# Pad tiles that move the addresses of matmul operands in a two-layer fp32r backbone

## The chip, the cores and the metric

The kernel runs on one core of a Trainium2 chip. The metric is the device time of one execution in microseconds; less is better. Below, PE is the matrix engine, and PEld is the load of a matmul's stationary operand into it, which the profile lists as an engine of its own. DVE and ACT are the vector and the scalar engine, POOL is GpSimd, and SP is the engine whose queue issues most weight transfers.

## What is computed

Two layers of a post-norm transformer backbone over 256 latent tokens of 2048 channels, with 256 context tokens that only the first layer reads. Layer 0 mixes tokens by neighbourhood attention with 16 heads, layer 1 by a gated MLP with a 128x128 position mix per channel group. A SwiGLU feed-forward block with an inner width of 5632 follows each mixer, and every sub-layer is modulated by shift, scale and gate vectors that are computed from a condition vector. In short:

```python
for i in range(2):
    sh1, sc1, g1, sh2, sc2, g2 = split(silu(c) @ ada_w[i] + ada_b[i], 6)
    a = h * (1 + sc1) + sh1
    y = attention(a, ctx) if i == 0 else gmlp(a)
    h = layer_norm(ALPHA * h + g1 * y)
    m = h * (1 + sc2) + sh2
    gate, up = split(m @ ffn_w_in[i], 2)
    h = layer_norm(ALPHA * h + g2 * ((silu(gate) * up) @ ffn_w_out[i]))
```

All of it is in float32. The kernel keeps that precision by splitting each operand of a large product into two fp32r parts (`hi`, the rounded value, and `lo`, the rest) and adding three products.

## The kernel before

**Products.** `mm3` (lines 88 to 91) issues three matmuls into one PSUM tile: stationary high with moving high (L89), stationary high with moving low (L90), stationary low with moving high (L91). In the blocks after attention the moving operand is 512 columns of a weight tile, and the stationary operand is 128x128 of the activations, split in the same way.

**Pieces.** All weights come through one queue of pieces of 128x1024 floats, in the order in which they are needed. `prefetch` (from line 106) loads a piece by SP's queue into one of four `raw` tiles, and `split_into` (L94 on ACT, L95 on DVE) writes its `hi` and `lo` tiles. There are two sets of these: set A, three pairs in the pool `outer`, and set B, two pairs in the pool `main`, which opens after attention. Pieces go round them by their number modulo 5: three pieces to A, then two to B. At the end of each output projection four half-tiles of a tile called `extra` (`extra_o`, `extra`, `extra_g`) take the place of A and B for the last two of its pieces and for two of the next block's.

**Blocks after attention.** One piece feeds 12 matmuls (two 128-deep slices, two halves of the tokens, three products). In `block_T` (feed-forward input: tiles `pg` and `pu`; gMLP input: `gv` and `gu`) the stationary operand is the modulated activation in `main` (tags `acth`, `actl`; tiles `f0h`, `m1h`, `f1h` and their low parts). In `project_out` (tiles `powo`, `pod`, `pogo`) it is a freshly split 128x256 slice in `outer` (tags `gh`, `gl`). `flip` (L768) transposes the feed-forward's inner activations by four small matmuls at a time. The feed-forward input has 11 blocks of two parts of eight pieces per layer, 176 pieces; the feed-forward output has 88 per layer, the gMLP input 64, and the two mixers' output projections 32 each.

**Fillers.** Between pieces `tick` starts tasks that compute the modulation vectors on DVE from transfers issued by ACT's queue (`ad` at L153, `ag` at L177).

**Addresses.** A pool gives each tag a place that is as large as its largest tile, one after the other in the order of first use, in steps of 32 bytes; pools lie on top of each other as they open. An address here is the byte offset within each partition. In the program of the kernel before:

```
pool   tag or tile             address            modulo 256   modulo 512
outer  xT (extra)              20032              64           64
outer  hi/lo, set A            60992 + n * 4096   64           64
outer  gh, gl                  110144 + n * 1024  64           64
main   h_t (16384 bytes)       118336             64           64
main   ca, cb, st (640 bytes)  134720
main   hi/lo, set B            135360 + n * 4096  192          192
main   acth, actl              155840, 172224     192          192
above  pw: w (extra_o)         192832             64           320
above  ffn: gTb, then sg       192832, 221504     64           320, 320
above  gm: ws, bs              192832, 201024     64           320
above  gm: vv (extra_g)        201088             128          384
```

The slices that a matmul of the blocks after attention reads start at whole multiples of 512 bytes within their tile, so the tile's remainder is the operand's. During attention the weights come from A alone, and the stationary or moving activations lie at 64 modulo 256 too. `ident`, the other operand of the transposes, is at 17408 (0 modulo 256).

Of the kernel before, what the change touches and what calls it, by code (L numbers as in the profile page):

```python
# [12 lines left out]
F32 = mybir.dt.float32  # L13
# [7 lines left out]
P = 128  # L21
# [31 lines left out]
def hybrid_kernel(ctx: ExitStack, tc: tile.TileContext, i, out):  # L53
# [34 lines left out]
    def mm3(ps, sh, sl, mh, ml, first, last, keep=lambda ins: ins):  # L88
        keep(T.matmul(ps, sh, mh, start=first, stop=False))  # L89
        keep(T.matmul(ps, sh, ml, start=False, stop=False))  # L90
        keep(T.matmul(ps, sl, mh, start=False, stop=last))  # L91
# [36 lines left out]
    def piece():  # L128
        prefetch(1)
        got = ready.pop(0)  # L130
        prefetch(pos["bufs"] - 1)
        return got

    def take(k):
        prefetch(k)
        got = ready[:k]
        del ready[:k]
        return got
# [41 lines left out]
    def act_split(src, name, at=None):  # L180
        if at is not None:
            split_into(at[0], at[1], src)
            return at
        gh = outer.tile([P, NT], F32R, tag="gh", name=f"gh{name}", bufs=4)
        gl = outer.tile([P, NT], F32R, tag="gl", name=f"gl{name}", bufs=4)
        split_into(gh, gl, src)
        return gh, gl
# [29 lines left out]
    def tick(n=1.0):  # L217
        fetch_ahead()
        if side:
            side.pop(0)()  # L220
            n *= BUSY
        state["credit"] += n * state["rate"] if tasks else 0.0
        while tasks and state["credit"] >= tasks[0][1]:
            state["credit"] -= tasks[0][1]
            pop_task()
        if not tasks:
            state["credit"] = 0.0

    def need(*keys):
        while any(t[0] in keys for t in tasks):  # L230
            pop_task()
# [46 lines left out]
    with tc.tile_pool(name="attnX", bufs=1) as px, ExitStack() as late:  # L278
# [148 lines left out]
        def acc_tile(name):  # L427
            return mp.tile([P, 512], F32, tag="acc", name=name, bufs=4)

        def s_tile(name):  # L430
            return mp.tile([P, 512], F32, tag="s", name=name, bufs=2)
# [120 lines left out]
    main = ctx.enter_context(tc.tile_pool(name="main", bufs=1))  # L552
    pos["wide"] = main
    pos["bufs"] = 5
    h_t = main.tile([P, 2, D], F32, tag="h", name="h_t")
    nc.sync.dma_start(h_t, i["x_tok"])

    def act_tiles(name):
# [5 lines left out]
    def stats_tile(name):  # L564
        return main.tile([P, 2, NB, 6], F32, tag="st", name=f"st{name}", bufs=2)

    def residual(ps, b, nb, g, st, name):
        sl = slice(nb * 512, (nb + 1) * 512)
        tmp = main.tile([P, 512], F32, tag="tmp", name=f"y{name}{b}{nb}", bufs=2)
        V.tensor_tensor(tmp, ps, g[:, sl], ALU.mult)  # L570
        V.scalar_tensor_tensor(h_t[:, b, sl], h_t[:, b, sl], ALPHA, tmp, ALU.mult, ALU.add)
        V.bn_stats(st[:, b, nb, :], h_t[:, b, sl])
# [12 lines left out]
    def preload_sqrt(st):  # L585
        S.activation(warm, st[:, 0, 0, 0:1], AF.Sqrt)
# [75 lines left out]
    def project_out(kts, src, key, name, finish, extra, last=False):  # L662
        st = stats_tile(name)
        hold = LAST if last else HOLD
        for nh in range(2):
            if nh == 0:
                ps = [[acc_tile(f"po{name}{nh}{n}{b}") for b in range(2)] for n in range(2)]
            else:
                ps = [[s_tile(f"po{name}{nh}0{b}") for b in range(2)]]
                ps.append([acc_tile(f"po{name}{nh}1{b}") for b in range(2)])  # L670

            def products(kt, x, w, n, b):
                c, tb = slice(n * 512, (n + 1) * 512), slice(b * P, (b + 1) * P)
                mm3(ps[n][b], x[0][:, tb], x[1][:, tb], w[0][:, c], w[1][:, c], kt == 0, kt == kts - 1)

            def fetch(kt, n):
                xs = []
                for k in range(n):
                    at = None
                    if k >= START:  # L680
                        if k % 2 == 0:
                            e = outer.tile([P, 4, NT], F32R, tag="ada", name=f"e{name}{k}", bufs=ADA)
                        at = e[:, 2 * (k % 2), :], e[:, 2 * (k % 2) + 1, :]
                    xs.append(act_split(src(kt + k), f"{name}{nh}_{kt + k}", at))
                return xs, take(n)

            k0 = 0
            if nh == 1:
                xs, ws = fetch(0, START)
                for n in range(2):  # L690
                    for j in range(START):
                        for b in range(2):
                            products(j, xs[j], ws[j], n, b)
                preload_sqrt(st)
                k0 = START
            k1 = kts - hold if nh == 1 else kts
            for kt in range(k0, k1):
                if nh == 1 and kt == max(k1 - 9, k0):
                    pos["extra"] = extra()
                w = piece() if nh == 0 or kt < k1 - START else take(1)[0]  # L700
                x = act_split(src(kt), f"{name}{nh}_{kt}")
                for n in range(2):
                    for b in range(2):
                        products(kt, x, w, n, b)
                if nh == 0 or kt < k1 - QUIET:
                    tick()
            if nh == 0:
                need(key)
                g = gate[key]
                for n in range(2):  # L710
                    for b in range(2):
                        residual(ps[n][b], b, n, g, st, name)
            else:
                xs, ws = fetch(k1, hold)
                for b in range(2):
                    for n in range(2):
                        for j in range(hold):
                            products(k1 + j, xs[j], ws[j], n, b)
                        with tc.high_priority(AHEAD):
                            residual(ps[n][b], b, 2 + n, g, st, name)  # L720
                    if not last:
                        with tc.high_priority(AHEAD):
                            finish(b, st)
                if last:
                    for b in range(2):
                        finish(b, st)
# [25 lines left out]
    def ffn(layer, m, key, name, finish, free, last=False):  # L752
# [41 lines left out]
    m = Modulated(0, 0, SH2, SC2, "f0")  # L794
    free = ExitStack()
    pw = free.enter_context(tc.tile_pool(name="pw", bufs=1))
    project_out(
        KT, lambda k: oT[:, k, :], (0, G1), "wo", m.first,
        lambda: pw.tile([P, 4, 1024], F32R, tag="w", name="extra_o"),
# [21 lines left out]
    pg = free.enter_context(tc.tile_pool(name="gm", bufs=1))  # L821
    ws = pg.tile([P, NH, P], F32, tag="ws", name="ws")
    nc.sync.dma_start(ws, i["w_s"])
    bs = pg.tile([P, NH], F32, tag="bs", name="bs")
    nc.sync.dma_start(bs, i["b_s"])
    vv = pg.tile([P, 2, D], F32, tag="vv", name="vv")
    st = stats_tile("v")
    for nb in range(NB):
# [173 lines left out]
```

## Time and profile before

| What | Value |
|---|---|
| time, median of 3 runs | 2493.1 us (2491.81 to 2497.22) |
| the profiled execution's own time | 2484.16 us |
| its span, first to last instruction | 2482.4 us |
| PE busy | 2409.0 us, 97% |
| PEld busy | 1976.3 us, 80% |
| DVE, ACT busy | 1754.9 us (71%), 1118.9 us (45%) |
| mean granted clock of PE | 0.992 |

Busy time of PE is no measure of its pace: matmuls are pipelined, so each one's recorded duration (about 0.39 us for 512 columns) overlaps the next one's. The pace is read from the distance between starts. The 2484.16 us stand 1.8 us above the span, and 0.36% under the median of the runs.

### The profile page before, as it was taken

Reading aid. Unit: us, or ns where it says so; the run is one execution under the profiler, and the core shown is the slowest. Engines: PE = TensorE matmul, PEld = TensorE weight load, DVE = VectorE, ACT = ScalarE, POOL = GpSimd, SP = SyncE. Lnnn points to the kernel's source line nnn. Section 1 sums busy time; section 2 is a strip of 40 time slices with the busy share of each in tenths; the row PEclk is TensorE's granted clock in tenths of the full one; section 3 lists DMA queues with packets and bytes.
Section 4 is the critical chain, followed back from the end, with each engine's and each line's share of the span. In section 5 each row is a group of like instructions: output and inputs, shape, how many; then the busy total and the mean of one; then the engine's idle time right before and its main releaser. Section 6 shows DMA issues by size and latency. Waiting matters only on the chain. (4 is left out here: it accounts for less than half of the span.)

```text
span 2482.4 us, 31276 instructions
## 1 busy us (share of the span) xinstructions
PE 2409.0 (97%) x11574; PEld 1976.3 (80%) x11574; DVE 1754.9 (71%) x2159; ACT 1118.9 (45%) x1534; POOL 110.5 (4%) x56
## 2 busy tenths in 40 slices
PE   6999899999999999999999999999999999999998
PEld 5787788888778888888888778777888888888886
DVE  3878877776877676666778778778755555566666
ACT  3344434345554444444455554446544444445453
POOL 0000200000010020000000020020100000020000
PEclk8999999999999999999999999999999999999999
DMA  8977787777568878888888767765676666666563
GB/s 328 347 258 253 243 285 269 268 269 240 184 225 299 283 272 287 280 285 291 283 290 278 255 211 259 255 205 184 214 228 224 218 222 226 220 196 190 174 208 131
DMA packets 167394, 610.57 MB, mean 246 GB/s; under 512 B 18916, under 2 KB 21284, under 8 KB 162884
## 3 DMA queue, kind: packets, MB, share of 16 engines
q1 hardware_dynamic: 120888, 440.64, 53.5%
q10 hardware_dynamic: 46224, 167.89, 19.6%
q8 instruction: 90, 1.47, 0.2%
q14 instruction: 64, 0.52, 0.1%
q0 software_dynamic: 128, 0.03, 0.0%
HBM read 606.40 MB, written 2.10 MB: 245 GB/s over the span
## 5 line engine op out<-in xcount | busy, mean ns | idle before, releaser
L94 ACT CAST hwf<-rwf 128x1024 fp32r<-128x1024 f32 x320 | 335.7, 1049 | 505.6 <-PE pu L91 228.5
L95 DVE TENSOR_TENSOR lwf<-rwf,hwf 128x1024 fp32r<-128x1024 f32 x320 | 405.5, 1276 | 194.2 <-ACT hwf L94 193.3
L153 DVE SCALAR_TENSOR_TENSOR ad<-ad,c_bc 128x1024 f32<-128x1024 f32 x192 | 234.0, 1222 | 169.8 <-DMA ad<-in_ada_t 169.2
L91 PE MATMUL pod<-hwd,gld 128*128 128x512 f32 x684 | 267.9, 392 | 0.7 <-DVE gld L95 0.7
L89 PE MATMUL pod<-hwd,ghd 128*128 128x512 f32 x684 | 268.2, 392 | 0.0
L90 PE MATMUL pod<-lwd,ghd 128*128 128x512 f32 x684 | 267.8, 392 | 0.0
L95 DVE TENSOR_TENSOR lwd<-rwd,hwd 128x1024 fp32r<-128x1024 f32 x172 | 211.5, 1231 | 52.4 <-ACT hwd L94 51.9
L177 DVE SCALAR_TENSOR_TENSOR gate<-ag,c_col,gate 128x1024 f32<-128x1024 f32 x128 | 164.3, 1287 | 108.8 <-DMA ag<-in_ada_g 108.5
L94 ACT CAST hwd<-rwd 128x1024 fp32r<-128x1024 f32 x172 | 179.9, 1046 | 26.2 <-PE pu L91 17.2
L91 PEld LDWEIGHTS pod<-hwd,gld 128*128 128x128 f32 x684 | 128.3, 188 | 29.6 <-DVE gld L95 1.1
L90 PEld LDWEIGHTS pod<-lwd,ghd 128*128 128x128 f32 x684 | 128.4, 188 | 28.5
L89 PEld LDWEIGHTS pod<-hwd,ghd 128*128 128x128 f32 x684 | 128.4, 188 | 28.5
L89 PE MATMUL pg<-hwf,f0h 128*128 128x512 f32 x320 | 127.5, 398 | 0.0
L89 PE MATMUL pg<-hwf,f1h 128*128 128x512 f32 x320 | 127.5, 398 | 0.0
L91 PE MATMUL pg<-hwf,f1l 128*128 128x512 f32 x320 | 125.8, 393 | 0.0
L91 PE MATMUL pg<-hwf,f0l 128*128 128x512 f32 x320 | 125.8, 393 | 0.0
L90 PE MATMUL pg<-lwf,f0h 128*128 128x512 f32 x320 | 125.7, 393 | 0.0
L90 PE MATMUL pg<-lwf,f1h 128*128 128x512 f32 x320 | 125.7, 393 | 0.0
L91 PE MATMUL pu<-hwf,f0l 128*128 128x512 f32 x320 | 125.7, 393 | 0.0
L91 PE MATMUL pu<-hwf,f1l 128*128 128x512 f32 x320 | 125.7, 393 | 0.0
L90 PE MATMUL pu<-lwf,f0h 128*128 128x512 f32 x320 | 125.7, 393 | 0.0
L89 PE MATMUL pu<-hwf,f1h 128*128 128x512 f32 x320 | 125.7, 393 | 0.0
(341 smaller groups left out, 5341.9 us busy)
## 6 DMA issues: line engine op xcount, KB each, us to landing
rwf<-in_w_in_t SPq DMA_DIRECT2D x320, 512.0 KB
ad<-in_ada_t ACTq DMA_DIRECT2D x192, 512.0 KB
rwd<-in_w_out SPq DMA_DIRECT2D x176, 512.0 KB
ag<-in_ada_g ACTq DMA_DIRECT2D x128, 512.0 KB
rwg<-in_w_gin SPq DMA_DIRECT2D x64, 512.0 KB
ap<-in_ada_p SPq DMA_DIRECT2D x19, 1024.0 KB
rwq<-in_w_q SPq DMA_DIRECT2D x32, 512.0 KB
rwo<-in_w_o SPq DMA_DIRECT2D x32, 512.0 KB
```

The lines of the kernel that those rows point to most:

```text
L89: keep(T.matmul(ps, sh, mh, start=first, stop=False))
L90: keep(T.matmul(ps, sh, ml, start=False, stop=False))
L91: keep(T.matmul(ps, sl, mh, start=False, stop=last))
L94: S.copy(hi, src)
L95: V.tensor_tensor(lo, src, hi.bitcast(F32), ALU.subtract)
L153: V.scalar_tensor_tensor(r, r, 1.0, c_bc[:, half * 1024 : (half + 1) * 1024], ALU.mult, ALU.mult, accum_out=o[:, nt : nt + 1],)
L177: V.scalar_tensor_tensor(g, loaded.pop(key), c_col[:, kt, 0:1], g, ALU.mult, ALU.add)
```

## The change

Three tiles that nothing reads or writes are added: 128 bytes in `main` behind `h_t`, 128 bytes in `pw` ahead of `extra_o`, and 64 bytes in `gm` between `bs` and `vv`. No instruction is added or removed.

```diff
@@ -553,6 +553,7 @@
     pos["wide"] = main
     pos["bufs"] = 5
     h_t = main.tile([P, 2, D], F32, tag="h", name="h_t")
+    main.tile([P, 32], F32, tag="pad", name="pad_main")
     nc.sync.dma_start(h_t, i["x_tok"])
@@ -794,6 +795,7 @@
     m = Modulated(0, 0, SH2, SC2, "f0")
     free = ExitStack()
     pw = free.enter_context(tc.tile_pool(name="pw", bufs=1))
+    pw.tile([P, 32], F32, tag="pad", name="pad_pw")
     project_out(
@@ -823,6 +825,7 @@
     bs = pg.tile([P, NH], F32, tag="bs", name="bs")
     nc.sync.dma_start(bs, i["b_s"])
+    pg.tile([P, 16], F32, tag="pad", name="pad_gm")
     vv = pg.tile([P, 2, D], F32, tag="vv", name="vv")
```

By the table above this puts B, `acth` and `actl` at 64 modulo 256 (320 modulo 512), `extra_o` and `extra_g` at 64 (64), `ws` at 192 and `sg` at 192.

## Rows read from the trace of the kernel before

**Rows 1.** The page's first two parts: busy time and share of the span by engine with the number of instructions; then, in 40 equal slices, the granted clock of PE and the rate of all transfers.

```profile
PE 2409.0 (97%) x11574; PEld 1976.3 (80%) x11574; DVE 1754.9 (71%) x2159; ACT 1118.9 (45%) x1534; POOL 110.5 (4%) x56
...
PEclk8999999999999999999999999999999999999999
...
GB/s 328 347 258 253 243 285 269 268 269 240 184 225 299 283 272 287 280 285 291 283 290 278 255 211 259 255 205 184 214 228 224 218 222 226 220 196 190 174 208 131
```

**Rows 2.** Waits of PE on other engines, the whole span: us in total, times, longest.

```profile
PE sp L846 <- DVE u L847: 4.7, 3, 2.7
...
PE gu L90 <- DVE lwg L95: 1.8, 1, 1.8
```

**Rows 3.** Timeline of PE in the feed-forward output of layer 0 (`pod`; stationary at 64 modulo 256): start us, duration us, instruction. From 1208.07 three pieces of set A, 36 matmuls; from 1216.24 two pieces of set B, 24 matmuls; from 1221.83 set A again.

```profile
1208.07 0.39 PE L89 MATMUL pod<-hwd,ghd 128*128 128x512 f32 x1
...
1209.21 0.39 PE L91 MATMUL pod<-hwd,gld 128*128 128x512 f32 x1
...
1216.24 0.40 PE L89 MATMUL pod<-hwd,ghd 128*128 128x512 f32 x1
...
1221.83 0.39 PE L89 MATMUL pod<-hwd,ghd 128*128 128x512 f32 x1
```

**Rows 4.** The same view in the feed-forward input of layer 0 (`pu`; stationary at 192 modulo 256). From 939.64 three pieces of A, 36 matmuls; from 948.03 two pieces of B, 24 matmuls; at 953.48 A again.

```profile
939.64 0.40 PE L89 MATMUL pu<-hwf,f0h 128*128 128x512 f32 x1
...
948.03 0.39 PE L89 MATMUL pu<-hwf,f0h 128*128 128x512 f32 x1
...
953.48 0.40 PE L89 MATMUL pg<-hwf,f0h 128*128 128x512 f32 x1
```

**Rows 5.** Timeline of all engines in the B stretch of rows 3: a matmul and the load of the next one's stationary operand, which runs under it.

```profile
1218.10 0.40 PE L91 MATMUL pod<-hwd,gld 128*128 128x512 f32 x1
1218.10 0.19 PEld L89 LDWEIGHTS pod<-hwd,ghd 128*128 128x128 f32 x1
```

**Rows 6.** Timeline of PE in the attention's V projection, where all operands lie at 64 modulo 256: first and last of a run of 37 matmuls.

```profile
475.68 0.39 PE L89 MATMUL vps<-hwv,ah 128*128 128x512 f32 x1
...
483.83 0.39 PE L89 MATMUL vps<-hwv,ah 128*128 128x512 f32 x1
```

**Rows 7.** Timeline of PE in two output projections, the third of six matmuls on one of the `extra` tiles and, four matmuls later, the first behind the six: `extra_o` (320 modulo 512 against a stationary operand at 64), then `extra` (64 against 64).

```profile
668.15 0.39 PE L91 MATMUL powo<-extra_o,glwo 128*128 128x512 f32 x1
...
669.05 0.40 PE L89 MATMUL powo<-hwo,ghwo 128*128 128x512 f32 x1
...
1417.43 0.39 PE L91 MATMUL pod<-extra,gld 128*128 128x512 f32 x1
...
1418.34 0.40 PE L89 MATMUL pod<-hwd,ghd 128*128 128x512 f32 x1
```

**Rows 8.** Timeline of PE behind a flip in the feed-forward input: four transposes, then 12 matmuls of set A, then the next four transposes; and the same with 12 matmuls of set B.

```profile
917.01 0.48 PE L89 MATMUL pg<-hwf,f0h 128*128 128x512 f32 x1
...
919.88 0.60 PE L768 MATMUL gt<-ident,sg 128*128 128x128 f32 x4
...
962.23 0.47 PE L89 MATMUL pg<-hwf,f0h 128*128 128x512 f32 x1
...
965.08 0.60 PE L768 MATMUL gt<-ident,sg 128*128 128x128 f32 x4
```

**Rows 9.** Timeline of ACT in the stretch of rows 3: the casts that write the `hi` tiles of four pieces in a row, which reach both sets.

```profile
1211.09 1.05 ACT L94 CAST hwd<-rwd 128x1024 fp32r<-128x1024 f32 x1
...
1213.81 1.04 ACT L94 CAST hwd<-rwd 128x1024 fp32r<-128x1024 f32 x1
...
1216.53 1.04 ACT L94 CAST hwd<-rwd 128x1024 fp32r<-128x1024 f32 x1
...
1219.31 1.04 ACT L94 CAST hwd<-rwd 128x1024 fp32r<-128x1024 f32 x1
```

**Rows 10.** Groups of PE's transposes on `sg` and on `u` (128 modulo 256) by line, tiles and shape: count, busy us, mean ns of one, idle before.

```profile
L768 PE MATMUL gt<-ident,sg 128*128 128x128 f32 x176 | 26.5, 272 | 0.0
...
L851 PE MATMUL uvt<-ident,u 128*128 128x128 f32 x32 | 6.1, 277 | 0.0
```

**Rows 11.** Busy time by stretch, in this order: feed-forward input and output of layer 0, the second half of the gMLP input, the gMLP output. Columns: us, busy us of PE, PEld, DVE, ACT and POOL with counts, granted clock, DMA share, GB/s.

```profile
677.50:1179.30 501.80, 500.14 (x2215) 406.52 (x2216) 355.55 (x384) 221.58 (x256) 24.14 (x11) 1.00 0.81 277
1179.50:1424.80 245.30, 244.50 (x1073) 199.41 (x1072) 194.72 (x286) 122.94 (x181) 0.00 (x0) 1.00 0.82 278
...
1525.30:1624.80 99.50, 94.68 (x417) 76.12 (x416) 76.43 (x90) 44.44 (x52) 6.65 (x6) 1.00 0.73 243
1625.70:1723.10 97.40, 94.68 (x422) 75.97 (x420) 79.13 (x97) 48.24 (x72) 12.78 (x1) 1.00 0.59 194
```

**Rows 12.** Waits of ACT's casts in the feed-forward input, whole span: us in total, times, longest.

```profile
ACT hwf L94 <- PE pu L91: 228.5, 141, 1.8
...
ACT hwf L94 <- DMA rwf<-in_w_in_t: 52.1, 22, 6.5
```

**Rows 13.** The chain that ended last, pieces of it in the gMLP stages: start us, us, what.

```profile
1567.02 5.67 DMA ag<-in_ada_g
...
1641.04 6.15 DMA ag<-in_ada_g
...
1649.62 9.36 DVE glgo L95
```

## The prediction

> **What bounds the kernel now.** The first view to read is the page's table of engines: PE is busy 97% of the span, and its clock is granted at nine tenths or more in every slice but the first [rows 1]; in most of the stretches looked at below it is 1.00, the 2.4 GHz level [rows 11]. Next are the waits of PE: in the blocks after attention they are a few microseconds [rows 2]. So the pace of PE's own stream sets the end, and the third view, the timeline of PE, is where it can be read: the distance from one start to the next, not the recorded duration.
>
> The timeline shows two paces for the same instruction. In the output projection of the feed-forward, 36 matmuls on set A take 1216.24 - 1208.07 = 8.17 us, 227 ns each; the next 24, on set B, take 5.59 us, 233 ns each [rows 3]. That alone could be a matter of the pool. But in the feed-forward input it is the other way about: A, 36 in 8.39 us, is the slow one at 233 ns, and B, 24 in 5.45 us, is fast at 227 ns [rows 4]. What goes with the pace in both is the remainder of the addresses: in the output the stationary operand is at 64 modulo 256 (A 64, B 192), in the input at 192 (A 64, B 192). Equal remainders are fast, remainders 128 apart slow. Attention, where everything lies at 64, is fast throughout: 36 matmuls in 8.15 us, 226 ns [rows 6]. While one matmul streams its moving operand, the next one's stationary operand is being loaded [rows 5], so two reads that could disturb each other run side by side; that this is the mechanism is a reading, the two paces are rows.
>
> The Trainium skill speaks against it. "TensorE: Matmul & The Clock Gate", in its step-by-step part, gives PE two independent read ports, one for the moving operand and one for the stationary, and says that loading the next weights takes no read bandwidth from the running matmul; "SBUF — State Buffer", under who interferes with whom, has PE wait for nobody. By that rule the offsets of the two operands could not matter, and the change would be worth nothing. This case's rows disagree, 227 against 233 ns.
>
> **The change part by part.** It adds, removes and moves no instruction and no transfer; it moves addresses. The 128 bytes in `main` take B and the activations from 192 to 64, which makes equal the A pieces of the input blocks and the B pieces of the output blocks, and leaves equal what was. The pads in `pw` and `gm` do the same for `extra_o` and `extra_g`.
>
> The gain, by cycles of five pieces (3 A and 2 B, 60 matmuls). An undisturbed equal stretch is the tail of A in the output projection: from 1209.21 to 1216.24 there are 31 matmuls in 7.03 us, 226.8 ns [rows 3], so a cycle with all operands equal takes 60 x 226.7 = 13.60 us (226.7 between this and attention's 226.4). A cycle of the output blocks takes 8.17 + 5.59 = 13.76 us now, 0.16 more; one of the input blocks 8.39 + 5.45 = 13.84 us, 0.24 more. This counts the first matmuls behind a slow stretch too, which are still late: from 1208.07 to 1209.21 five take 228 ns each.
>
> - Feed-forward input: 176 pieces per layer less 2 on `extra` tiles is 34.8 cycles, 69.6 for two layers, x 0.24 = 16.7 us.
> - gMLP input: 62 pieces, 12.4 cycles x 0.24 = 3.0 us.
> - Feed-forward output: 86 pieces per layer, 34.4 cycles x 0.16 = 5.5 us.
> - The mixers' output projections: 30 pieces each, 12 cycles x 0.16 = 1.9 us.
> - Pieces on `extra` tiles with unequal remainders: eight, 96 matmuls x 6 ns = 0.6 us.
>
> That is 27.7 us. Two things come off.
>
> First, not every stretch is steady. Behind a flip's four transposes 12 matmuls of A take 919.88 - 917.01 = 2.87 us, and 12 of B, with equal remainders, 965.08 - 962.23 = 2.85 us [rows 8]: there the equal ones are late as well, and almost nothing is won. Two layers have 44 flips with 12 matmuls behind each; 3 in 5 are on A, 6 ns each: 44 x 12 x 0.6 x 6 ns = 1.9 us of the sum above that will not come. Bounds: 0, if these starts settle sooner, and 1.9.
>
> Second, in the gMLP stages the chain leaves PE for transfers and DVE several times, 5.67 and 6.15 us on gate weights and 9.36 us on splits [rows 13]. PE that comes there earlier may only wait longer. At risk is what is gained ahead of the last such place, the 3.0 us of the gMLP input and part of its output; I take half, 1.5 us, with bounds of 0 and 3.5.
>
> What moves with the pads beside the products: the casts into A and B take 1.04 to 1.05 us alike [rows 9], so ACT's writes cost the same at either address, and DVE's splits, which read the same tiles, are taken to do so too. Transposes from `sg` (64) and `u` (128) take 272 and 277 ns [rows 10]: 208 of these small matmuls with `sg` and `u` moved are worth 1 us at most either way, taken as nothing. The spatial products pass from a distance of 64 to one of 128: 32 matmuls, under 0.3 us at 6 ns. The pads issue nothing, so no queue and no wait changes; what hides the supply of weights stays: ACT's casts wait for PE to free a buffer for 228.5 us in `pu`, and for the transfer itself 52.1 us [rows 12].
>
> Sum: 27.7 - 1.9 - 1.5 = 24.3, say 24 us. By the bounds of the two deductions it is 22 to 28, and 21 if the transposes and the spatial products cost their full 1.3 us besides. The profiled execution would fall from 2484.2 to 2460 us. The runs' median stands 9 us above that execution; the matmuls' pace is the same in both as far as the clock is granted, so the same 24 us come off it: 2493.1 - 24 = 2469 us.
>
> **The rivals.**
>
> *The addresses don't set the pace, or the pads get no place.* If the pace goes with something else that differs between the stretches, or if an unused tile takes no room, no matmul gets faster and the time stays at 2493. The rule of the two ports in the Trainium skill's TensorE page, above, would have it so. Against the first: A and B swap roles when only the stationary operand moves [rows 3, 4]. It would need another property that swaps in the same way. Chance 0.04.
>
> *The period is 512 bytes, not 256.* After the change the remainders modulo 256 are equal, but modulo 512 A (64) and the activations (320) stand 256 apart, as do B (320) and `gh` (64). That is 3 in 5 of the input blocks' 410 pieces and 2 in 5 of the output blocks' 232, about 4,070 matmuls, as many as are slow now. Before the change all equal pairs on A and B are equal modulo 512 as well, so rows 3 and 4 can't tell. If 256 apart costs as much as 128 apart, nothing is won (2493); if it costs over 1.2 ns more per matmul (5 us / 4,070), that is past 234.3 ns, the kernel is slower; at the 239 ns of the disturbed matmuls behind a flip [rows 8] it is 4,070 x 6 ns = 24 us slower, 2517. Against it stands one place: `extra_o` at 320 against `gh` at 64, where four matmuls take 0.90 us, as four on `extra` (64 against 64) take 0.91 [rows 7], while four at the slow pace of rows 3 take 0.93. It is a short stretch. Chance 0.02 for as slow as now, 0.03 for slower.
>
> *Supply takes it back.* In layer 0's feed-forward the transfers run at 277 and 278 GB/s with a DMA share of 0.81 and 0.82, against 243 and 194 GB/s in the gMLP [rows 11]. A pace 1.7% higher (0.24 of 13.84) wants 282. If 278 were all that is to be had, layer 0's 8.4 + 2.8 us would be lost beside the 1.5, and 13 us be left: 2480. Against it: slices of the page reach 299 and 347 GB/s, and casts wait for PE more than for transfers [rows 12]. Chance 0.05.
>
> **How the numbers follow.** The forecast has 0.86, with its own range of 2462 to 2475: 21 to 28 us off, and 2.7 us on either side for the runs, which span 5.4 us. A measurement of this kernel tells 0.2% (5 us) from no change. Faster by more: 0.86 + 0.05 = 0.91. Within: 0.04 + 0.02 = 0.06. Slower: 0.03. The range must leave out at most 2 in 10; with the rivals outside, 0.14 is out already, so it takes the forecast's range with more room on both sides, since the 9 us between the runs and the profiled execution are not explained: 2460 to 2479.
>
> **What would show it.** In the trace of after, the starts of `pod` on B and of `pu` on A should stand 227 ns apart, a cycle of five pieces should take 13.6 us in both, and the feed-forward inputs should be shorter by 7 to 8 us each, the outputs by 2.5 to 3. ACT's and DVE's durations should be the same. If A in `pu` and B in `pod` stay at 233 ns, or others turn slow, the period is not 256. If the pace is 227 but waits of PE on `lwf` or `lwd` appear, it is supply; if the gMLP stages alone give nothing, the second deduction was too small. Most likely to make the number wrong is the runs' offset to the profiled execution, which no view explains.

## The result and the profile after

The changed kernel takes 2464.23 us (median of 4 runs, 2457.31 to 2465.89) beside 2492.45 us for the kernel before (2486.06 to 2497.22): a ratio of 0.989 with a 95% interval of 0.9866 to 0.9914. A second set of runs, the changed kernel once more in the last experiment below, gave 2472.7 us and 0.9915 (0.9886 to 0.9943). The forecast was 2469 us.

The timeline of PE after the change, read as in [rows 3] and [rows 4]: first the feed-forward input of layer 1, with three pieces of set A from the first row and two of set B from the second; then the feed-forward output of layer 1, in the same order.

```profile
1739.47 0.39 PE L89 MATMUL pu<-hwt,f1h 128*128 128x512 f32 x1
...
1747.63 0.39 PE L89 MATMUL pu<-hwt,f1h 128*128 128x512 f32 x1
...
1753.07 0.39 PE L89 MATMUL pu<-hwt,f1h 128*128 128x512 f32 x1
...
2252.89 0.39 PE L89 MATMUL pod<-hwd,ghd 128*128 128x512 f32 x1
...
2261.05 0.39 PE L89 MATMUL pod<-hwd,ghd 128*128 128x512 f32 x1
...
2266.49 0.39 PE L89 MATMUL pod<-hwd,ghd 128*128 128x512 f32 x1
```

In both blocks 36 matmuls on A take 8.16 us and 24 on B take 5.44 us: 226.7 ns each, wherever they read. The slow pace is gone. Over all start distances under 300 ns between such matmuls, joined to the addresses in each program, the kernel before has a mean of 227.7 ns where the operands' remainders are equal (5007) and 233.0 ns where they are 128 apart (3848); the changed kernel has 227.0 ns (9166, all equal). The recorded duration hardly tells it: 0.39 us, where it was 0.39 or 0.40 before (group means in `pu` of 389 ns for 393). The distance of the starts shows the change.

Busy time by stretch of the kernel after: the feed-forward input and output of layer 0, the gMLP with its output projection, the feed-forward input and output of layer 1. Columns as in [rows 11].

```profile
672.00:1165.40 493.40, 491.68 (x2215) 406.44 (x2216) 353.82 (x382) 221.80 (x256) 26.05 (x11) 1.00 0.82 280
1165.70:1413.90 248.20, 243.39 (x1073) 200.51 (x1071) 196.07 (x288) 123.89 (x181) 0.00 (x0) 0.99 0.81 277
...
1415.80:1709.20 293.40, 282.65 (x1248) 229.47 (x1248) 235.25 (x277) 147.06 (x202) 33.32 (x20) 0.99 0.69 230
...
1709.20:2203.00 493.80, 492.10 (x2216) 406.54 (x2217) 295.01 (x267) 222.47 (x256) 24.18 (x11) 1.00 0.68 221
2203.00:2443.10 240.10, 240.10 (x1064) 198.63 (x1063) 159.66 (x200) 117.27 (x173) 5.39 (x2) 1.00 0.57 181
```

The first row answers to the 501.80 us of [rows 11], and is 8.4 us shorter with the same matmuls. The second answers to 245.30 us there and is longer by 2.9. The kernel before has for the other three:

```profile
1426.80:1725.10 298.30, 286.37 (x1248) 229.52 (x1248) 236.40 (x277) 146.98 (x202) 33.33 (x20) 0.99 0.68 226
...
1725.10:2227.20 502.10, 500.46 (x2216) 406.74 (x2217) 294.14 (x267) 221.80 (x256) 25.07 (x11) 1.00 0.67 218
2227.20:2470.10 242.90, 242.90 (x1064) 198.82 (x1063) 159.44 (x200) 116.86 (x173) 5.39 (x2) 1.00 0.57 179
```

Layer 1's feed-forward, where PE waits for almost nothing, gives 8.3 and 2.8 us. The profiled execution fell by 26.9 us, from 2484.16 to 2457.31. 4.6 us of that were ahead already when the first output projection began (first `powo` after attention at 582.4 and 577.8 us on the traces), and in attention the change moves no operand; such differences come between executions of one kernel too (below).

The longer second row has one place. The timeline of DVE, then of PE, at the head of that stage:

```profile
1165.66 0.68 DVE L783 TENSOR_TENSOR sg<-pu,sg 128x512 f32<-128x512 f32 x1
1169.55 1.22 DVE L153 SCALAR_TENSOR_TENSOR ad<-ad,c_bc 128x1024 f32<-128x1024 f32 x1 [3.21 <-DMA ad<-in_ada_t]
...
1171.84 0.68 DVE L783 TENSOR_TENSOR sg<-pu,sg 128x512 f32<-128x512 f32 x1
...
1172.58 0.50 PE L89 MATMUL pod<-hwd,ghd 128*128 128x512 f32 x1 [4.13 <-DVE sg L783]
```

DVE stands for 3.21 us at a modulation task whose tile has not landed. The feed-forward's second multiplication is queued behind it (L783 at 1171.84), and PE, which needs its result and the buffers behind it, waits 4.13 us. Whether the faster pace made this wait is asked in the last experiment.

### The profile page after: what moved, and what is told of

The parts are those of the page before. It is cut to its first block, busy times and chain, and to the rows that moved or that the text cites. A ratio compares the mean times of both kernels' runs of the same rounds, so it can differ in the third digit from the quotient of the medians.

```text
span 2455.5 us, 31276 instructions
## 1 busy us (share of the span) xinstructions
PE 2381.3 (97%) x11574; PEld 1975.5 (80%) x11574; DVE 1754.1 (71%) x2159; ACT 1121.0 (46%) x1534; POOL 111.4 (5%) x56
## 5 line engine op out<-in xcount | busy, mean ns | idle before, releaser
L89 PE MATMUL pod<-hwd,ghd 128*128 128x512 f32 x684 | 267.1, 390 | 4.1 <-DVE sg L783 4.1
L91 PE MATMUL pod<-hwd,gld 128*128 128x512 f32 x684 | 266.8, 391 | 0.5 <-DVE gld L95 0.5
L90 PE MATMUL pod<-lwd,ghd 128*128 128x512 f32 x684 | 266.5, 390 | 0.0
L89 PEld LDWEIGHTS pod<-hwd,ghd 128*128 128x128 f32 x684 | 128.7, 188 | 31.2 <-DVE sg L783 4.6
L91 PEld LDWEIGHTS pod<-hwd,gld 128*128 128x128 f32 x684 | 128.6, 188 | 27.9 <-DVE gld L95 0.9
L90 PEld LDWEIGHTS pod<-lwd,ghd 128*128 128x128 f32 x684 | 128.7, 188 | 26.4
L89 PE MATMUL pg<-hwf,f1h 128*128 128x512 f32 x320 | 126.4, 395 | 0.0
L89 PE MATMUL pg<-hwf,f0h 128*128 128x512 f32 x320 | 126.4, 395 | 0.0
L91 PE MATMUL pg<-hwf,f1l 128*128 128x512 f32 x320 | 124.7, 390 | 0.0
L91 PE MATMUL pg<-hwf,f0l 128*128 128x512 f32 x320 | 124.7, 390 | 0.0
L89 PE MATMUL pu<-hwf,f0h 128*128 128x512 f32 x320 | 124.5, 389 | 0.0
L90 PE MATMUL pu<-lwf,f0h 128*128 128x512 f32 x320 | 124.5, 389 | 0.0
L91 PE MATMUL pu<-hwf,f0l 128*128 128x512 f32 x320 | 124.5, 389 | 0.0
L89 PE MATMUL pu<-hwf,f1h 128*128 128x512 f32 x320 | 124.5, 389 | 0.0
L90 PE MATMUL pu<-lwf,f1h 128*128 128x512 f32 x320 | 124.5, 389 | 0.0
L91 PE MATMUL pu<-hwf,f1l 128*128 128x512 f32 x320 | 124.5, 389 | 0.0
```

## The experiments

The theory: a 512-column fp32r matmul takes 226.7 ns from start to start where its moving operand and the stationary operands loaded around it have equal addresses modulo 256, and about 233 ns where they have not. Rivals: moving the pools as such helps; set A, set B or `main` is slow in itself; changing remainders from piece to piece costs, not the distance between the two operands; only a distance of 128 clashes. For the size of the result: late transfers take back a part of it.

### Moving everything, but by a whole period

```diff
     h_t = main.tile([P, 2, D], F32, tag="h", name="h_t")
+    main.tile([P, 64], F32, tag="pad", name="pad_main")
```

> The kernel before with 256 bytes of pad behind h_t and nothing else: every tile from set B on is moved, and more pool is taken than in the change, but all remainders modulo 256 stay as they were. If the remainders set the pace: time as before (ratio 0.997 to 1.003), A in the feed-forward input and B in its output at 233 ns, input stage 501 to 502 us. If moving the pools as such (other places, other overlaps of tiles) is what helped: ratio near 0.99.

Measured: 2488.78 us, ratio 0.9995 (0.9975 to 1.0015): no change. Layer 1's feed-forward in its trace:

```profile
1730.70:2234.00 503.30, 501.86 (x2217) 407.95 (x2218) 293.70 (x267) 221.73 (x256) 24.11 (x11) 1.00 0.65 217
2234.00:2476.90 242.90, 242.90 (x1065) 198.74 (x1063) 159.60 (x201) 116.82 (x173) 5.39 (x2) 1.00 0.55 179
```

The input is as slow as before and the output has the same 242.90 us. More pool and other places are not what helps; the remainder is.

### Set A alone to the other remainder

```diff
+            if m == 0:
+                outer.tile([P, 32], F32, tag="pad0", name="pad_0")
             hi = pool.tile([P, 1024], F32R, tag="hi" + tag, name=f"h{name}", bufs=bufs)
             lo = pool.tile([P, 1024], F32R, tag="lo" + tag, name=f"l{name}", bufs=bufs)
+            if m == 0:
+                outer.tile([P, 32], F32, tag="pad1", name="pad_1")
```

> The kernel before with 128 bytes of pad ahead of set A and 128 behind it, so that A alone goes to 192 modulo 256; main, gh, gl and attention's tiles keep their remainders. If the remainders set the pace, the stages trade places: attention's matmuls on A, all fast before, turn slow (V projection 233 ns for 226.4), the feed-forward inputs turn fast (493 us each for 502, A and B both at 227 ns), the feed-forward outputs turn slow throughout (A and B both at 233 ns: 1032 matmuls x 6.3 ns = 6.5 us over the 240 to 242 of an equal one, some 248). In all some 4,370 unequal pairs of 512 columns for 4,140: about as slow as before, ratio 0.998 to 1.005, more if the 256-column matmuls of the Q projection slow down too (768 x some ns). If set A itself or main itself were slow or fast, attention would not change.

Measured: 2493.19 us, ratio 1.0003 (0.999 to 1.0017). Layer 1's feed-forward, input and output, and a run of 23 matmuls of the V projection in attention:

```profile
1733.50:2229.50 496.00, 494.46 (x2216) 407.79 (x2217) 293.70 (x267) 221.80 (x256) 23.45 (x11) 1.00 0.66 220
2229.50:2476.50 247.00, 247.00 (x1064) 198.84 (x1063) 159.84 (x201) 116.68 (x173) 5.40 (x2) 1.00 0.55 176
```

```profile
478.02 0.39 PE L89 MATMUL vps<-hwv,ah 128*128 128x512 f32 x1
...
483.13 0.40 PE L90 MATMUL vps<-lwv,ah 128*128 128x512 f32 x1
```

The stages traded places, under an unchanged total: the input is fast (496.0 for 502.1 us), the output slower than it ever was (247.0 for 242.9), and the V projection takes 5.11 us for 22 starts, 232 ns, where [rows 6] has 226. No set is slow in itself.

### Equal remainders in the outputs, unequal ones throughout the inputs

```diff
 (the changed kernel, in act_tiles)
+        main.tile([P, 32], F32, tag="padx", name="pad_x" + name)
         return (
             main.tile([P, KT, NT], F32R, tag="acth", name=name + "h"),
```

> The changed kernel with 128 more bytes ahead of the activations' tiles in main: B stays at 64, the activations go back to 192. The input blocks then have unequal remainders on A and on B, the output blocks equal ones on both. If the remainders set the pace: feed-forward input 493.4 + 2112 x 6.3 ns = 506 to 507 us each, slower than in the kernel before (501.8), with 233 ns on A and B alike; feed-forward output of layer 1 239.7 us as in after; in all about 5 us slower than before, ratio 1.000 to 1.004. If it is the two sets' being in different remainders that costs (a change from piece to piece), not the distance to the stationary operand: inputs as slow as before at most, 500 to 502 us.

Measured: 2494.45 us, ratio 1.001 (0.999 to 1.003). Layer 1's feed-forward, then three starts in its input (A from the first, B from the second):

```profile
1731.20:2238.40 507.20, 505.34 (x2216) 406.61 (x2217) 294.01 (x267) 221.90 (x256) 23.60 (x11) 1.00 0.65 216
2238.40:2478.80 240.40, 240.40 (x1064) 198.68 (x1063) 159.60 (x200) 117.09 (x173) 5.39 (x2) 1.00 0.56 180
```

```profile
1762.28 0.40 PE L89 MATMUL pu<-hwt,f1h 128*128 128x512 f32 x1
...
1770.67 0.40 PE L89 MATMUL pu<-hwt,f1h 128*128 128x512 f32 x1
...
1776.28 0.40 PE L89 MATMUL pu<-hwt,f1h 128*128 128x512 f32 x1
```

36 matmuls on A in 8.39 us and 24 on B in 5.61 us, 233 and 234 ns, though A and B have the same remainder now; the stage's 507.2 us are 13.4 above the changed kernel's, for the 2112 x 6.3 ns = 13.3 us forecast. It is the distance to the stationary operand that costs, not a change between pieces.

### Other distances

Four more kernels have 32, 64, 96 or 192 bytes in the place of the 256 of the first edit (`[P, 8]`, `[P, 16]`, `[P, 24]`, `[P, 48]`).

> The kernel before with 32 bytes behind h_t: B and the activations at 224 modulo 256, so the distance moving minus stationary is -160 (96) on A in the input blocks and +160 (-96) on B in the output blocks, while B with the activations and A with gh stay equal. If only distance 0 modulo 256 is fast: 233 ns there, inputs 501 to 502 us. If the cost follows how far apart they are: between 227 and 233. If 128 is the one bad distance (a period of 256 with a single clash): 227 ns, inputs 493 us.

> The kernel before with 64 bytes behind h_t: B and the activations at 0 modulo 256, distance 64 on A in the input blocks and -64 (192) on B in the output blocks. Only 0 is fast: about 233 ns (the few matmuls on extra_g at distance 64 in the kernel before took 229 to 236), inputs 501 us. By distance: some 230 ns. One bad distance of 128: 227 ns and 493 us. A period of 64 bytes: 227 ns as well.

> The kernel before with 96 bytes behind h_t: B and the activations at 32 modulo 256, distance 32 on A in the input blocks and -32 (224) on B in the output blocks. Only 0 is fast: about 233 ns, inputs 501 us. By distance: 227 to 229 ns. One bad distance of 128: 227 ns and 493 us.

> The kernel before with 192 bytes behind h_t: B and the activations at 128 modulo 256. The run with 64 bytes showed an asymmetry: the moving operand 64 bytes past the stationary one (A in the input blocks) took 229.4 ns, 64 bytes short of it (B in the output blocks) 233.3 ns. Here the signs are exchanged: A in the input blocks is 64 short, B in the output blocks 64 past. If the sign of the distance decides: inputs at 233 ns and 502 us, outputs at 229.4 ns on B, some 241.3 us for layer 1's. If it is the kind of block that decides (which operand is the activation): inputs 229.4 ns and 499 us, outputs 233.3 ns and 243 us.

The pace of an unequal stretch in layer 1, 36 matmuls on A in the input and 24 on B in the output, worked out from the starts in each trace:

| distance, moving minus stationary, modulo 256 | ns per matmul | where |
|---|---|---|
| 0 | 226.7 | the changed kernel, everywhere |
| 32 | 233.4 | 96 bytes of pad, inputs |
| 64 | 229.4 and 229.6 | 64 bytes, inputs; 192 bytes, outputs |
| 96 | 233.7 | 32 bytes, inputs |
| 128 | 233.1 and 233.0 | the kernel before, inputs and outputs |
| 160 | 234.0 | 32 bytes, outputs |
| 192 | 233.3 and 233.3 | 192 bytes, inputs; 64 bytes, outputs |
| 224 | 233.5 | 96 bytes, outputs |

The rows of the one odd value: with 64 bytes of pad the input on A (8.25 us for 36) and the equal stretch on B behind it (5.49 us for 24), then that input stage as a whole; last, with 192 bytes, the output on B (5.51 us for 24).

```profile
1758.10 0.40 PE L89 MATMUL pu<-hwt,f1h 128*128 128x512 f32 x1
...
1766.35 0.40 PE L89 MATMUL pu<-hwt,f1h 128*128 128x512 f32 x1
...
1771.84 0.40 PE L89 MATMUL pu<-hwt,f1h 128*128 128x512 f32 x1
```

```profile
1727.60:2226.40 498.80, 497.16 (x2217) 406.62 (x2218) 293.64 (x267) 221.77 (x256) 22.70 (x11) 1.00 0.66 219
```

```profile
2268.52 0.40 PE L89 MATMUL pod<-hwd,ghd 128*128 128x512 f32 x1
...
2274.03 0.40 PE L89 MATMUL pod<-hwd,ghd 128*128 128x512 f32 x1
```

Of the eight distances tried only 0 is at 226.7 ns. The cost doesn't grow with the distance: 32 bytes cost what 128 do. The equal stretches beside them in the inputs, on B and the activations at 0, 32, 128, 192 and 224 modulo 256, take 227 to 229 ns, so it is the difference that counts and not the remainder itself. A moving operand 64 bytes past the stationary one is the exception, and by its sign: 64 short of it costs the full price, in either kind of block. In the stretch itself 64 past costs 2.7 to 2.9 ns a matmul instead of 6.3 to 7.3, but the equal stretch behind it is late as well, 229 ns, and by stage the price is three fifths: layer 1's input takes 498.8 us, 5.0 above the changed kernel's, and the kernel before 8.3 above. So with 192 bytes layer 1's output took 242.4 us and not the 241.3 expected. The times of the single runs (2496.81, 2483.54, 2489.22 and 2493.76 us, beside 2490.74, 2490.74, 2490.74 and 2497.33 for the kernel before) can't carry this; the starts do.

### One of the three stationary loads

```diff
 (the changed kernel, in act_tiles)
-        return (
-            main.tile([P, KT, NT], F32R, tag="acth", name=name + "h"),
-            main.tile([P, KT, NT], F32R, tag="actl", name=name + "l"),
-        )
+        xh = main.tile([P, KT, NT], F32R, tag="acth", name=name + "h")
+        main.tile([P, 32], F32, tag="padl", name="pad_l" + name)
+        return xh, main.tile([P, KT, NT], F32R, tag="actl", name=name + "l")
```

> The changed kernel with 128 bytes between the activations' high tile and their low tile: of the three stationary loads of a product only the low part (L90) is at 192, moving operands on A and B at 64. If the next load is what disturbs the running matmul, the slow place is the matmul ahead of the one with the low part (L91, in the order in which these issue), one start distance in three of the triple, some 2 ns per matmul on average, inputs 493.4 + 704 x 6.3 ns = 498 us. If a matmul is slowed by its own stationary operand's place, the slow one is L90 itself; the stage's time is the same. The trace's order of starts tells which.

The expectation names the lines in the wrong order: the matmul with the low stationary part is L91, and the one ahead of it, under which that part is loaded, L90. The starts in the feed-forward input of layer 0:

```profile
940.21 0.39 PE L89 MATMUL pu<-hwf,f0h 128*128 128x512 f32 x1
940.43 0.40 PE L90 MATMUL pu<-lwf,f0h 128*128 128x512 f32 x1
940.66 0.40 PE L91 MATMUL pu<-hwf,f0l 128*128 128x512 f32 x1
940.90 0.39 PE L89 MATMUL pu<-hwf,f0h 128*128 128x512 f32 x1
```

Neither reading alone holds. Over some 700 such starts each in the `pu` blocks, the distance behind L89 is 226.7 ns, behind L90 232.5 and behind L91 234.2: both the matmul under which the unequal part is loaded and the one that uses it are late. One unequal load in three costs 5.8 + 7.5 = 13.3 ns, nearly twice the 6.6 ns per matmul of a stream in which all are unequal. So the stage took 502.7 us, not the 498 forecast (2480.8 us in all, a single run). Behind L90 the running matmul's own stationary part is equal to its moving operand and only the part loaded under it is not; behind L91 it is the other way about. Each is about as late as a matmul for which both are unequal (233 ns), so in this stream one of the two is enough, and both together cost no more. Why is open. That a late matmul passes its lateness on does not fit: L89, which comes behind L91, is on time, and the first matmuls behind a slow stretch in [rows 3] are late by some 1 ns each, not by 7.

### Whether late transfers take part of the gain

The changed kernel once more:

> The changed kernel once more, unaltered. What is asked: the trace of after has one stall that the kernel before has not, 4.5 us at the head of layer 0's feed-forward output, where DVE sits behind a modulation task (L153) whose transfer lands late, and the matmuls behind it run some microseconds slowly; that stage took 248.2 us where 242.4 were forecast. If a faster PE makes this stall (supply gives back part of the gain), it is here again and the stage takes 247 to 249 us. If it is chance of one execution, the stage takes 242 to 244 us. The pace of the 512-column matmuls is 226.8 ns on either reading; ratio to the kernel before 0.987 to 0.992.

The kernel before once more:

> The kernel before, unaltered, for a second look at its stalls. If the faster pace makes the stall at the head of layer 0's feed-forward output (stalls there 3.5 us in before, 9.1 and 11.5 in after), this stage has 3 to 5 us of stalls again and takes some 247 us from its first matmul to the gMLP's first. If it is chance, any value up to 8 us, as in the run with 256 bytes of pad, can come.

Both kernels with half of each modulation task left out:

```diff
-        tc.keep_in_program_order(nc.scalar.dma_start(r, src))
+        tc.keep_in_program_order(nc.scalar.dma_start(r[:, :512], src[:, :512]))
...
-                r, r, 1.0, c_bc[:, half * 1024 : (half + 1) * 1024], ALU.mult, ALU.mult,
+                r[:, :512], r[:, :512], 1.0, c_bc[:, half * 1024 : half * 1024 + 512], ALU.mult, ALU.mult,
```

(and the same cut in `gate_task`).

> The kernel before with half of each modulation task left out: of the 1024 columns of every ad and ag tile only 512 are loaded and multiplied (84 MB of transfers less, and some 200 us of DVE), so its output is another. It is the floor to compare the next run with. If late tasks make the stalls of PE in layer 0's feed-forward output and in the gMLP (23.7 us over the four stages in the trace of before), these fall below 12 us and the kernel is 10 us or more under the kernel before. The pace stays at 227 and 233 ns.

> The changed kernel with the same half of each modulation task left out. The pace alone is worth 27 us by the two traces, but only 20 to 28 us came in the runs. If supply gives part of it back, the difference to the run on the halved kernel before is the whole 27 us, and its stalls in the four stages equal that kernel's. If what is missing is chance, or lies elsewhere, the difference is 20 to 25 us, and stalls differ as much as before.

The changed kernel's second set of runs is 2472.7 us, the single run of the kernel before 2487.66 us, the halved pair 2471.25 us (ratio to the kernel before 0.992, 0.9901 to 0.9938) and 2448.94 us (0.9834, 0.9811 to 0.9856): 22.3 us between the two. By the traces, first matmul of a stage to the first of the next, in us (one execution each):

| stage | before | again | after | again | halved before | halved after |
|---|---|---|---|---|---|---|
| attention (from PE's first matmul) | 575.6 | 576.3 | 571.6 | 576.1 | 564.7 | 563.6 |
| output projection of attention | 95.1 | 95.1 | 94.2 | 94.2 | 95.1 | 94.2 |
| feed-forward input, layer 0 | 502.0 | 502.2 | 493.7 | 495.1 | 502.9 | 494.9 |
| feed-forward output, layer 0 | 247.3 | 247.0 | 250.1 | 252.4 | 248.1 | 244.8 |
| gMLP with its projection | 298.3 | 301.4 | 293.4 | 302.3 | 293.7 | 294.8 |
| feed-forward input, layer 1 | 502.1 | 502.2 | 493.8 | 493.9 | 503.4 | 494.3 |
| feed-forward output, layer 1 | 242.9 | 243.0 | 240.1 | 240.1 | 242.9 | 240.3 |

Rows of the halved pair, the feed-forward output of layer 0 and the gMLP, the kernel before first:

```profile
1169.00:1417.10 248.10, 244.85 (x1073) 199.46 (x1071) 176.73 (x289) 125.21 (x186) 0.48 (x1) 1.00 0.71 234
1417.10:1710.80 293.70, 284.00 (x1248) 228.47 (x1248) 222.12 (x277) 145.93 (x202) 33.54 (x20) 0.99 0.62 201
```

```profile
1159.00:1403.80 244.80, 241.58 (x1074) 199.55 (x1072) 177.31 (x289) 124.99 (x186) 0.57 (x1) 1.00 0.72 237
1403.80:1698.60 294.80, 282.98 (x1249) 230.41 (x1249) 221.48 (x277) 146.57 (x202) 34.77 (x20) 0.98 0.61 200
```

*The stalls.* They are counted as what is over 227 ns at each start distance above 250 ns. The expectation for the halved kernel before failed here: in the feed-forward output of layer 0 and the gMLP its stalls are 4.3 + 15.9 us, against 3.5 + 20.9 in the kernel before, and not below 12 together. The largest part of what it gains lies in attention, 575.6 to 564.7 us.

*The feed-forward output of layer 0.* With half of the tasks the stage gives its gain, 248.1 to 244.8 us, which fits late tasks holding it up; it rests on one execution of each. That the faster pace makes them late is not shown. PE stalls there for 9.1 and 11.5 us in the two traces of the changed kernel and for 3.5 and 3.3 in the two of the kernel before, which looks like it; but kernels with a slow input show 8.3 (256 bytes of pad) and 8.4 us (192 bytes) too, and the six other kernels with whole tasks 4.0 to 6.8, among them the one with A moved, whose input is fast, with 6.0. The stall comes and goes at either pace; the two highest values are the changed kernel's. Whether its pace has a part in it is open.

*The gMLP.* The halved pair doesn't bring the whole 27 us: it loses 1.1 us there, where the pace should give 4. But the stage scatters by more than that from execution to execution: 293.4 and 302.3 us in the two traces of the changed kernel, 295.8 (256 bytes of pad) to 301.4 at the pace of the kernel before. The chain that ended last in the gMLP of the halved changed kernel still leaves PE for weights and gate weights, as in [rows 13]:

```profile
1530.87 6.48 DMA rwg<-in_w_gin
1537.48 5.77 DMA ag<-in_ada_g
...
1592.95 5.23 DMA ag<-in_ada_g
```

So that PE arrives earlier and waits longer, as the second deduction said, fits the halved pair, where its stalls in this stage are 15.9 and 20.8 us. How much of the stage's gain this takes is not shown.

## Why the prediction was right

**What bounds the kernel, and the two paces.** Right. The pace of PE's stream set the end, and the swap of roles between [rows 3] and [rows 4] was the distance of the remainders: the kernel with a whole period of pad, the one with A moved and the one with the activations moved back agree with it in size. The Trainium skill's page "TensorE: Matmul & The Clock Gate", in its step-by-step part, has the loading of the next weights take no read bandwidth from the running matmul. The measurement decides against what the prediction drew from it, that the addresses could not matter: 226.7 against 233.1 ns with nothing but addresses changed. One reading was too light: the waits after attention are not a few microseconds in all, as [rows 2] seemed to say, but 24.4 us of stalls in layer 0's output and the gMLP alone, and it is in these stages that the gain is not seen for certain.

**The cost by cycles.** 13.60 us for an equal cycle of five pieces was forecast, 8.16 + 5.44 = 13.60 us measured. The feed-forward inputs were forecast at 8.35 us each ahead of deductions and gave 8.3 and 8.3 (7.1 in the second trace of layer 0), layer 1's output 2.75 and gave 2.8, attention's output projection 0.95 and gave 0.9. Layer 0's output, with 2.75 forecast too, is the term that did not come: 250.1 and 252.4 us in the two traces of the changed kernel, for 247.3 and 247.0.

**The first deduction, 1.9 us for starts behind flips, failed.** In the changed kernel 12 matmuls behind a flip take 2.83 us, where [rows 8] has 2.87 and 2.85:

```profile
951.98 0.48 PE L89 MATMUL pg<-hwf,f0h 128*128 128x512 f32 x1
...
954.81 0.60 PE L769 MATMUL gt<-ident,sg 128*128 128x128 f32 x4
```

Over the 43 places of this kind that a trace holds, the mean fell from 2.864 to 2.827 us: 1.6 us came of the 1.9 that were taken off. The prediction read the 2.87 and 2.85 us as 12 late matmuls of 239 ns. Some 0.09 us of each is the first start distance, 0.31 to 0.32 us before and after; the eleven others took 232 ns on A and 231 on B, and take 228 after, settled by the fifth. Why they settle is open. The moved `sg`, which the prediction costed at nothing, was not moved by itself. With A moved alone, where all remainders of the matmuls are equal too but the operands lie at 192 and `sg` at 64, and not the other way about, the same 12 take 2.86 us (mean of 20); with 32, 64 and 96 bytes of pad, where `sg` lies at 96, 128 and 160, the equal ones take 2.85. Of the 2.2 us by which layer 1's input is longer with A moved (496.0 us for 493.8), 0.6 us are of these starts; 1.5 us are nine more start distances above 300 ns.

**The second deduction, 1.5 us for the gMLP, can't be judged.** The chain leaves PE there after the change too. Of the 4 us due nothing is seen in the halved pair, and a gain between -4 and +8 us in single traces of the full kernels: the stage's own spread is larger than the term.

**The rivals.** The period is not 512: in the changed kernel A in the inputs is 256 apart and B is not, and both take 226.7 ns. The four matmuls of [rows 7] on which that rested told it rightly. Supply as a ceiling of 278 GB/s is out: layer 0's input ran at 280 and gave its whole gain. In layer 0's output a late task took 4.1 us of PE's time in the trace shown above.

**The number.** 24 us were forecast; 28 came in the first set (medians), 20 in the second, 22 in the halved pair. What separates these is the spread of executions, attention alone 571.6 to 576.3 us on one or the other kernel's equal code. So the inputs and layer 1's output came as worked out, but that the total fell so near to 24 us is in part luck: in the first pair of traces attention gave 4.0 us that the change has no part in, and layer 0's output lost 2.9. The 9 us between the profiled execution and the median of the runs were of that kind: runs of the kernel before reached from 2481.1 to 2497.47 us in one comparison.

## What to carry to other kernels

Where PE is the bound, read the distance between starts of equal matmuls, not their durations, and group it by what may differ: here it showed two paces 3% apart that no group of the page separates. If they go with the operands' addresses, lay the tiles out so that moving and stationary operands of back-to-back fp32r matmuls of 512 columns are equal modulo 256 bytes; unused tiles of a few dozen floats do it. Expect the gain only in stages where PE itself ends last, and prove it with a pad of a whole period, which moves everything and must change nothing.

## What the runs showed of the hardware

- 36 matmuls in 8.16 us is 226.7 ns, 544 cycles at the 2.4 GHz that a granted clock of 1.00 means, and 36 in 8.40 us, as in the feed-forward outputs of the kernel with A moved, is 233.3 ns, 560 cycles: the two paces are 16 cycles apart.
- The cost is not symmetric: a moving operand 64 bytes past the stationary one costs 2.7 ns in the stretch itself, 64 bytes short 6.6; layer 1's input takes 498.8 and 502.6 us with them on A, 493.8 with equal operands.
- One unequal stationary load in three costs two matmuls' worth, 13.3 ns: the matmul under which it is loaded and the one that uses it are late.
- Matmuls of 256 columns don't show it: in the Q projection the start distance was 119.7 ns with equal remainders and 118.9 with A moved by 128 (means over the trace of distances under 200 ns).
